# Two conditioning parts of a two-block kernel, summed on VectorE and TensorE instead of on TensorE alone

## The chip, the cores and the metric

The kernel runs on one core of one Trainium2 chip. The metric is the device time of one execution in microseconds, lower is better. The kernel before takes 1520.97 us, the median of three runs from 1515.06 to 1523.17. The one execution that was profiled took 1522.59 us, and its first to last instruction span 1520.8 us.

## The reference, cut to what matters

Two transformer blocks are computed for 256 tokens of width 1024 in float32. Each layer is conditioned on a vector `c`: a row vector of 1024 is multiplied with a 1024 x 6144 matrix, and the six pieces of 1024 shift, scale and gate the layer's stages.

```python
c_act = jax.nn.silu(c)
mod = c_act @ w_ada[layer] + b_ada[layer]
shift_m, scale_m, gate_m, shift_f, scale_f, gate_f = [m[:, None, :] for m in jnp.split(mod, N_MOD, axis=-1)]
h = rmsnorm(x, norm_mix[layer]) * (1.0 + scale_m) + shift_m
x = x + gate_m * hybrid_mixer(h, ...)
h = rmsnorm(x, norm_ffn[layer]) * (1.0 + scale_f) + shift_f
x = x + gate_f * hierarchical_moe(h, ...)
```

The first block's mixer has a projection, three kinds of recurrences and an output projection; a mixture of experts follows. The second block has two layers: a state-space and dilated-attention mixer with a SwiGLU, then a convolution with a SwiGLU.

## The kernel before, in words

There are three conditioning products (index `l`: 0 for the first block, 1 and 2 for the layers of the second). Each is cut into three parts (`b`) of 2048 columns, and each part into eight slices (`kt`) of 128 rows, so a slice is a tile of 128 x 2048 floats, 1 MB. `ada` (L484) takes one slice: for each of four groups of 512 columns one matmul multiplies the slice with a column of `c` broadcast to 32 columns, and the four groups land in the four 32-row strips of one PSUM bank (L498), which eight slices accumulate. The profile counts each such float32 matmul as two records, so a slice is 8 records of L498. After the eighth slice ScalarE copies the bank out (`adasb`, L504) and `ada_end` transposes it and adds the bias, some steps later.

The slices come in through the same ring as all dense weights: the class `Weights` keeps a list of jobs in the order in which they will be used, each one a load of up to 1 MB into one of five buffers (`rawa`, NA = 5), issued on SyncE's queue (L183). `pump` issues job i as soon as job i-5 has been marked free in program order, and the buffer that it takes is the one that was freed first. All loads are in one queue, so a load that waits for its buffer holds back those behind it. A dense weight's buffer is freed once it has been split: for each unit (128 x 1024) ScalarE writes a rounded high part (`whi`, L211), VectorE the rest (`wlo`, L212). Four units fit (`n_whl` = 4), so splits normally run one or two units ahead of the matmuls; `pump_units` stops where the next unit's raw load has not been issued yet. An `ada` slice's buffer is freed by `ws.free` (L500), as soon as its matmuls have been written down.

The work of one dense block (two units, 128 output columns each) is issued by `dense_B` (matmuls L627 to L629) or `dense_A` (L701 to L703). Inside it, `tick` is called four times per block; each tick advances every generator in `pipes` by one step, and so spreads the recurrences, the norms and the conditioning's ends between the matmuls. At the end of a block, `after` runs the slices that `spread` put there.

The first mixer's blocks are `fg` (2), `gq` (3), `vt` (4, by `dense_A`), `rqk` (3), `gate` (4) and the output projection. Part (0, 1) has its slices 0 | 1, 2 | 3, 4 after the blocks gq0, gq1 and gq2, its slices 5, 6 after vt0 and 7 after vt1; parts (0, 2) and (1, 0) follow, mostly two slices to a block. The job list around the change runs gq1, slices 1 and 2, gq2, slices 3 and 4, vt0, slices 5 and 6, vt1, slice 7 and the first of (0, 2), vt2, and so on. Meanwhile the forget gates, the transposes of the log gates and the recurrences (`recur`, L931, exponentials at L939, score masks at L980 to L991) run from the ticks.

Part (1, 2) belongs to the attention stage: its eight slices come after the blocks 0, 2, 4, ... 14 of the 18 `qkv` blocks. In the first half of this stage GpSimd loads position-bias tiles (`bt`, L1789 and L1793) with many small packets.

Of the kernel before, what the change touches and what calls it, by code (L numbers as in the profile page):

```python
# [11 lines left out]
FT = mybir.dt.float32  # L12
FR = mybir.dt.float32r
I32 = mybir.dt.int32
AF = mybir.ActivationFunctionType
OP = mybir.AluOpType
# [248 lines left out]
def trace(tc, A, out, dbg=None, stop=None):  # L265
    with ExitStack() as ctx:
        _trace(ctx, tc, A, out, dbg, stop)


def _trace(ctx, tc, A, out, dbg, stop):  # L270
    nc = tc.nc
    V, S, G, P = nc.vector, nc.scalar, nc.gpsimd, nc.tensor

    const = ctx.enter_context(tc.tile_pool(name="const", bufs=1))
# [14 lines left out]
    def acc(tag="acc"):  # L289
        n, pool = psums[tag]  # L290
        return pool.tile([128, 512], FT, name=tag, tag=tag, bufs=n)

    def mis():
        return acc("mis")

    NA, NB, NW = 5, 9, 2
    ws = Weights(nc)
# [5 lines left out]
    ada_at = {}  # L303

    HALVED = {(2, 2)}

    def plan_ada(l, b, kt):
        w, c = ada_w[l], b * 2048
        if (l, b) in HALVED:
            h, q = divmod(kt, 4)  # L310
            src, shape = w[q * 256:q * 256 + 256, c + h * 1024:c + h * 1024 + 1024], (2, 1024)
            src = src.rearrange("(k p) n -> p k n", p=128)
        else:
            src, shape = w[kt * 128:(kt + 1) * 128, c:c + 2048], (2048,)
        ws.add(("ada", l, b, kt), [(None, src)], shape)
# [85 lines left out]
    wk = l1.enter_context(tc.tile_pool(name="wk1", bufs=1))  # L401
# [27 lines left out]
    ones_1 = epsc[:, 1:2]  # L429
# [45 lines left out]
    cs = const.tile([128, 16], FT, name="cs")  # L475
    ps = mis()
# [4 lines left out]

    ada_ps = {}

    def ada(l, b, kt):  # L484

        h = 2 if (l, b) in HALVED else 1
        half, q = divmod(kt, 8 // h)
        if q == 0:
            ada_ps[0] = pada.tile([128, 512], FT, name="adaps", tag="adaps", bufs=1)
        w = 512 // h  # L490
        ps = ada_ps[0][:, :w]
        raw = ws.get(("ada", l, b, kt))
        if h == 1:
            raw = raw[:, None]
        col = (0 if l == 0 else 8) + q * h
        for k in range(h):
            for g in range(4):
                P.matmul(ps[32 * g:32 * g + 32, :], cs[:, col + k:col + k + 1].to_broadcast([128, 32]),  # L498
                         raw[:, k, g * w:(g + 1) * w], start=(q + k == 0), stop=(q * h + k == 7))
        ws.free(("ada", l, b, kt))  # L500
        if not ada_ends(l, b, kt):
            return
        sb = const.tile([128, 512], FT, name="adasb", tag="adasb", bufs=1)
        S.activation(sb[:, :w], ps, AF.Copy)  # L504
        pipes.append(ada_end(l, b * 16 + half * 8, 4 // h, sb))

    def ada_ends(l, b, kt):

        return kt % (4 if (l, b) in HALVED else 8) == (3 if (l, b) in HALVED else 7)

    def ada_end(l, n, w, sb):
        bias = vcol["b_ada"] if l == 0 else vcol["ada_b_2"][:, 48 * l - 48:48 * l]
        for _ in range(5):
            yield True
        tp = mis()
        for j in range(w):
            P.transpose(tp[:, j * 128:(j + 1) * 128], sb[:, j * 128:(j + 1) * 128], ident)
        o = mods[l][:, n:n + 4 * w].rearrange("p (g j) -> p g j", g=4)
        V.tensor_tensor(o, tp[:, :128 * w].rearrange("p (j g r) -> p g j r", g=4, r=32)[:, :, :, 0],
                        bias[:, n:n + 4 * w].rearrange("p (g j) -> p g j", g=4), op=OP.add)  # L520


    pipes = []
# [25 lines left out]
    class Squares:  # L549
# [6 lines left out]
        def add(self, t, scale=1.0):  # L556

            self.todo.append((t, scale))
            while self.todo and (len(self.todo) > 1 or self.n == 7):
                if 1 < self.n < 7:  # L560
                    V.tensor_tensor(self.sum, self.sum, self.end[-1], op=OP.add)
                t, scale = self.todo.popleft()
                sq = const.tile([128, T], FT, name="sq", tag="sq", bufs=2) if self.n else self.sum
                S.activation(sq, t, AF.Square, scale=scale)
                self.end = self.end[-1:] + [sq]
                self.n += 1
# [7 lines left out]
    def rsqrt(ms, scale=1.0, w=2, v=None):  # L574


        y, t = (const.tile([128, 12], FT, name="nw", tag="nw", bufs=9)[:, :w] for _ in range(2))
        if v is None:
            v = const.tile([128, 12], FT, name="nw", tag="nw", bufs=9)[:, :w]
            V.tensor_scalar(v, ms, scale, EPS, op0=OP.mult, op1=OP.add)  # L580
        V.tensor_scalar(y.bitcast(I32), v.bitcast(I32), -0.5, 1597463007.0, op0=OP.mult, op1=OP.add)
        for _ in range(3):
            V.tensor_tensor(t, y, y, op=OP.mult)
            V.scalar_tensor_tensor(t, t, -0.5, v, op0=OP.mult, op1=OP.mult)
            V.scalar_tensor_tensor(y, t, 1.5, y, op0=OP.add, op1=OP.mult)
        return y
# [44 lines left out]
    def after(name, b):  # L631
        last = False
        for k in ada_at.get((name, b), ()):
            if last:
                later(1, lambda k=k: ada(*k))
            else:
                ada(*k)
            last = last or ada_ends(*k)
# [87 lines left out]
    for kt in range(4):  # L726
        ada(0, 0, kt)
    ps = mis()
# [67 lines left out]


    w01 = wk.tile([128, C1OFF - o0], FT, name="w01", tag="sg")
    nc.sync.dma_start(w01, A["consts"][:, o0:C1OFF])
    G.tensor_copy(wlev, w01)  # L800
    nc.sync.dma_start(l1c, A["consts"][:, C1OFF:C1END])
# [269 lines left out]
    sg = wk.tile([128, 8, T], FT, name="sg", tag="sg")  # L1071
# [49 lines left out]
    with ExitStack() as l1:  # L1121
        wk = l1.enter_context(tc.tile_pool(name="wkm", bufs=1, reuse_waits="tile"))
# [48 lines left out]
        for kt in range(8):  # L1171
            if kt == 3:
                ps = mis()
# [67 lines left out]
        ps = mis()  # L1241
# [307 lines left out]
    with ExitStack() as l2:  # L1549
        hl = l2.enter_context(tc.tile_pool(name="hl2", bufs=1, reuse_waits="tile"))  # L1550
        dr = l2.enter_context(tc.tile_pool(name="dr2", bufs=1, space=bass.MemoryType.DRAM))
        wk = l2.enter_context(tc.tile_pool(name="wk2", bufs=1, reuse_waits="tile"))
# [7 lines left out]
        def yslab(tag, dt=FT):  # L1560
            return wk.tile([128, 8, T], dt, name=tag, tag=tag, bufs=2)
# [92 lines left out]
        ylo = []  # L1654
        yhi = [yslab("yh8", FR) for _ in range(2)]
        bcT = wk.tile([128, 8, T], FT, name="bcT")
        cw = vcol[("hy_conv_w_2")]
        cbm = wk.tile([128, 4, 3, 128], FT, name="cbm")
        Ub = cc("Uk")
# [329 lines left out]
    with ExitStack() as l3:  # L1989
        hl = l3.enter_context(tc.tile_pool(name="hl3", bufs=1, reuse_waits="tile"))  # L1990
        wk = l3.enter_context(tc.tile_pool(name="wk3", bufs=1, reuse_waits="tile"))
# [92 lines left out]
        ps = mis()  # L2084
# [9 lines left out]
        r = rsqrt(dl[:, 2:4])  # L2094
# [4 lines left out]
        ps = mis()  # L2099
# [33 lines left out]
    with ExitStack() as lf_:  # L2133
        wk = lf_.enter_context(tc.tile_pool(name="wko", bufs=1, reuse_waits="tile"))
        ps = acc()
        sq.mean(ps)
        r = rsqrt(ps[:, 0:2])
# [21 lines left out]
```

## Time and profile before

| | |
|---|---|
| median of three runs | 1520.97 us |
| the profiled execution | 1522.59 us, span 1520.8 us |
| TensorE matmul / weight load busy | 89% / 76% |
| VectorE / ScalarE / GpSimd busy | 56% / 42% / 17% |
| HBM traffic | 344.83 MB read, 227 GB/s over the span |
| L498, all nine conditioning parts | 77.5 us of TensorE, 640 records |
| first mixer, dense blocks gq to gate | about 62 to 236 us |
| attention stage, blocks qkv0 to qkv17 | about 760 to 927 us |

Times in the rows are counted from the span's start. Busy time is the time in which an engine had at least one instruction of that kind running; a bracket behind a timeline row gives the idle time before it and what ended that. PEld is TensorE's weight load, PEclk the share of full clock that TensorE was granted.

### The profile page before, as it was taken

To read this page: it belongs to the slowest core of one execution; us is meant where nothing else is said; L and a number is where in the kernel's file an instruction comes from. 1 tells how busy PE (TensorE), PEld (TensorE's weight loads), DVE (VectorE), ACT (ScalarE), POOL (GpSimd) and SP (SyncE) were. 2 spreads that over 40 slices of the span, in tenths; PEclk is the share of its full clock that TensorE was granted. 3 is DMA by queue.
4 is the path that set the end of the run, shared out by engine and by line. 5 is a ranking of instruction groups with operands and counts; after the bars stand their busy time and mean duration, and the time that the engine had idled before them with its cause. 6 is when DMAs were issued, how large, how long until landed. Compare 5 with 4: busy or idle time off the path is not lost.

```text
span 1520.8 us, 29127 instructions
## 1 busy us (share of the span) xinstructions
PE 1348.5 (89%) x12025; PEld 1156.3 (76%) x12025; DVE 851.7 (56%) x1727; ACT 645.5 (42%) x1164; POOL 253.6 (17%) x321
## 2 busy tenths in 40 slices
PE   3989899677766797999998898999999998999997
PEld 1777679544333596878986786899998987899997
DVE  3655555512211587787655565665555777765553
ACT  2543233210000365665343554454443776554432
POOL 3100000100000201034165106700000574000000
PEclk9898999798888798999999999999999999999999
DMA  8885577699999975676899966776557554877540
GB/s 310 273 304 190 174 237 281 273 417 386 410 418 419 223 171 175 208 242 197 201 173 176 248 194 194 220 196 181 173 179 234 164 180 139 250 195 192 171 164 28
DMA packets 277756, 348.22 MB, mean 229 GB/s; under 512 B 18521, under 2 KB 250448, under 8 KB 258672
## 3 DMA queue, kind: packets, MB, share of 16 engines
q1 hardware_dynamic: 264704, 334.81, 69.1%
q0 software_dynamic: 12160, 9.56, 4.4%
q8 instruction: 97, 1.59, 0.5%
q10 hardware_dynamic: 752, 1.91, 0.3%
q14 instruction: 43, 0.35, 0.1%
HBM read 344.83 MB, written 1.13 MB: 227 GB/s over the span
## 4 chain that ended last, share of the span: by engine, by line
PE 49%; DMA 11%; DVE 6%; issue 4%; POOL 2%; ACT 2%; DVEq 0%; POOLq 0%; SPq 0%; ACTq 0%
PE acc L627 14%; PE acc L628 14%; PE acc L629 14%; DMA bt<-rbd 2%; DMA rawb<-in_expert_w_up_dram 2%; DMA rawa<-in_hy_w_in_dram 2%; DVE wlo L212 2%; PE adaps L498 2%; POOL c L2029 1%; DMA rawb<-in_expert_w_gate_dram 1%; DMA rawa<-in_expert_w_down_dram 1%; PE acc L1380 1%; DMA rawa<-in_expert_w_up_dram 1%; DMA rawa<-in_expert_w_gate_dram 1%; ACT whi L211 1%
## 5 line engine op out<-in xcount | busy, mean ns | idle before, releaser
L627 PE MATMUL acc<-hhi,whi 128*128 128x256 f32 (+2 forms) x1728 | 511.9, 296 | 9.1 <-ACT hhi L617 5.4
L212 DVE TENSOR_TENSOR wlo<-rawa,whi 128x1024 fp32r<-128x1024 f32 (+1 forms) x303 | 370.0, 1225 | 256.2 <-ACT whi L211 253.5
L628 PE MATMUL acc<-hlo,whi 128*128 128x256 f32 (+2 forms) x1728 | 498.2, 288 | 1.6 <-DVE hlo L623 1.2
L629 PE MATMUL acc<-hhi,wlo 128*128 128x256 f32 (+2 forms) x1728 | 496.0, 287 | 1.3 <-DVE wlo L212 1.3
L211 ACT ACTIVATE whi<-rawa 128x1024 fp32r<-128x1024 f32 (+1 forms) x304 | 313.1, 1034 | 150.1 <-PE acc L628 106.5
L627 PEld LDWEIGHTS acc<-hhi,whi 128*128 128x128 f32 (+2 forms) x1728 | 336.8, 195 | 43.9 <-issue 22.5
L628 PEld LDWEIGHTS acc<-hlo,whi 128*128 128x128 f32 (+2 forms) x1728 | 337.2, 195 | 6.4 <-DVE hlo L623 4.2
L629 PEld LDWEIGHTS acc<-hhi,wlo 128*128 128x128 f32 (+2 forms) x1728 | 337.2, 195 | 2.0 <-DVE wlo L212 1.7
L627 PE MATMUL acc<-ghi,whi 128*128 128x256 f32 x352 | 100.1, 284 | 0.0
L628 PE MATMUL acc<-glo,whi 128*128 128x256 f32 x352 | 99.6, 283 | 0.0
L629 PE MATMUL acc<-ghi,wlo 128*128 128x256 f32 x352 | 99.6, 283 | 0.0
L498 PE MATMUL adaps<-rawa,cs 128*32 128x512 f32 (+1 forms) x640 | 77.5, 589 | 6.0 <-DMA rawa<-in_w_ada_dram 6.0
L1380 PE MATMUL acc<-rawb,X 128*32 128x256 f32 x576 | 64.3, 453 | 19.1 <-DMA rawb<-in_expert_w_gate_dram 10.9
L1979 POOL TENSOR_SCALAR dg<-cst,pcols 128x128 f32<-128x128 f32 x75 | 53.7, 734 | 84.3 <-PE acc L629 84.3
L628 PEld LDWEIGHTS acc<-glo,whi 128*128 128x128 f32 x352 | 67.6, 192 | 0.0
L629 PEld LDWEIGHTS acc<-ghi,wlo 128*128 128x128 f32 x352 | 67.6, 192 | 0.0
L627 PEld LDWEIGHTS acc<-ghi,whi 128*128 128x128 f32 x352 | 67.5, 192 | 0.0
L1388 DVE TENSOR_TENSOR sq<-sq,acc 128x256 f32<-128x256 f32 x8 | 3.4, 420 | 114.2 <-PE acc L1380 114.2
L1380 PEld LDWEIGHTS acc<-rawb,X 128*32 128x32 f32 x576 | 28.0, 129 | 43.7 <-DMA rawb<-in_expert_w_gate_dram 16.4
L1380 PE MATMUL acc<-rawa,X 128*32 128x256 f32 x320 | 41.5, 451 | 21.5 <-DMA rawa<-in_expert_w_up_dram 11.4
L1793 POOL DMA_DIRECT2D bt<-rbd x64 | 51.0, 813 | 30.2 <-DMA bt<-rbd 30.1
L627 PE MATMUL acc<-yh,whi 128*128 128x256 f32 x192 | 54.8, 286 | 0.0
(597 smaller groups left out, 2179.3 us busy)
## 6 DMA issues: line engine op xcount, KB each, us to landing
rawa<-in_ada_w_dram SPq DMA_DIRECT2D x48, 1024.0 KB, 5.2
rawa<-in_w_ada_dram SPq DMA_DIRECT2D x24, 1024.0 KB, 8.3
rawa<-in_ffn_w_gate_dram SPq DMA_DIRECT2D x44, 512.0 KB, 4.1
rawa<-in_ffn_w_up_dram SPq DMA_DIRECT2D x44, 512.0 KB, 5.4
rawa<-in_hy_w_in_dram SPq DMA_DIRECT2D x20, 1024.0 KB, 5.5
rawa<-in_hy_w_in_dram SPq DMA_DIRECT2D x40, 512.0 KB, 7.7
rawb<-in_expert_w_gate_dram SPq DMA_DIRECT2D x18, 1024.0 KB, 19.9
rawb<-in_expert_w_up_dram SPq DMA_DIRECT2D x18, 1024.0 KB, 16.3
```

Of the source, the lines that this page charges most:

```text
L211: self.nc.scalar.activation(hv, src, AF.Copy)
L212: (engine or self.nc.vector).tensor_tensor(lv, src, hv.bitcast(FT), op=OP.subtract)
L498: P.matmul(ps[32 * g:32 * g + 32, :], cs[:, col + k:col + k + 1].to_broadcast([128, 32]), raw[:, k, g * w:(g + 1) * w], start=(q + k == 0) ...
L627: P.matmul(ps, wh, xh, start=start, stop=False)
L628: P.matmul(ps, wh, xl, start=False, stop=False)
L629: P.matmul(ps, wl, xh, start=False, stop=stop)
L1380: P.matmul(ps[32 * i:32 * i + 32, :256], X[:, kt, o:o + 32], half(raws[i], kt // 4)[:, kt % 4 * 256:kt % 4 * 256 + 256], start=(kt == 0), ...
L1388: V.tensor_tensor(hid, s, out_[1][:, :256], op=OP.mult)
L1793: nc.gpsimd.dma_start(bt[:, a, o + 64 * g:o + 64 * g + 64], bass.AP(tensor=rbd.tensor, offset=base + 511 + 127 * g, ap=[[0, 2], [1, 64], [ ...
L1979: G.tensor_scalar(diag[n][:, i], ident, tap(i, n), None, op0=OP.mult)
L2029: G.tensor_tensor(c2, c2, pr_, op=OP.add)
```

## The change

For the two parts (0, 1) and (1, 2) the sum over the 1024 rows is made in two steps. Each slice is multiplied by its column of `c`, as a per-partition scalar, and added into a 128 x 2048 float32 tile `asum` on VectorE, in four instructions of 512 columns (the first slice by `tensor_scalar`, the other seven by `scalar_tensor_tensor`, in place). The four instructions are steps of a generator, one to a tick, so that they fall into the block after the one that the slice stood behind, and `ws.free` of the slice's buffer follows the fourth. Two ticks after the last slice's fourth step, four matmuls with a column of ones, broadcast to 32 columns, sum `asum` over the partitions into a PSUM bank of the pool `mis`; the copy to `adasb` and `ada_end` are as before. `asum` takes the memory of the tag `sg` in the first mixer and of `bcT` in the attention stage. The other seven parts are unchanged.

```diff
     HALVED = {(2, 2)}
+    SUMMED = {(0, 1), (1, 2)}
...
+    def ada_summed(l, b, kt):
+
+        raw = ws.get(("ada", l, b, kt))
+        col = cs[:, (0 if l == 0 else 8) + kt:(0 if l == 0 else 8) + kt + 1]
+        if kt == 0:
+            asums[l, b] = asums[l, b]()
+        t = asums[l, b]
+
+        def add():
+            for g in range(4):
+                r = slice(g * 512, g * 512 + 512)
+                if kt == 0:
+                    V.tensor_scalar(t[:, r], raw[:, r], col, None, op0=OP.mult)
+                else:
+                    V.scalar_tensor_tensor(t[:, r], raw[:, r], col, t[:, r], op0=OP.mult, op1=OP.add)
+                if g < 3:
+                    yield True
+            ws.free(("ada", l, b, kt))
+            if kt < 7:
+                return
+            yield True
+            yield True
+            ps = mis()
+            for g in range(4):
+                P.matmul(ps[32 * g:32 * g + 32, :], ones_1.to_broadcast([128, 32]), t[:, g * 512:(g + 1) * 512], start=True,
+                         stop=True)
+            sb = const.tile([128, 512], FT, name="adasb", tag="adasb", bufs=1)
+            S.activation(sb, ps, AF.Copy)
+            pipes.append(ada_end(l, b * 16, 4, sb))
+        pipes.append(add())
+
     def ada(l, b, kt):
 
+        if (l, b) in SUMMED:
+            ada_summed(l, b, kt)
+            return
...
-        return kt % (4 if (l, b) in HALVED else 8) == (3 if (l, b) in HALVED else 7)
+        return (l, b) not in SUMMED and kt % (4 if (l, b) in HALVED else 8) == (3 if (l, b) in HALVED else 7)
...
+    asums[0, 1] = lambda wk=wk: wk.tile([128, 2048], FT, name="asum", tag="sg")
...
+        asums[1, 2] = lambda: wk.tile([128, 2048], FT, name="asum", tag="bcT")
```

## Rows read from the trace of the kernel before

**Rows 1.** The page's first part: busy time and share of each engine.
```profile
PE 1348.5 (89%) x12025; PEld 1156.3 (76%) x12025; DVE 851.7 (56%) x1727; ACT 645.5 (42%) x1164; POOL 253.6 (17%) x321
```

**Rows 2.** Busy time by stretch, first mixer; columns as the header row says.
```profile
core 0: us, PE busy (x) PEld busy (x) DVE busy (x) ACT busy (x) POOL busy (x), PEclk, DMA share, GB/s
70.00:84.00 14.00, 14.00 (x118) 10.82 (x118) 9.57 (x21) 8.06 (x12) 0.00 (x0) 1.00 0.72 266
84.00:94.00 10.00, 10.00 (x75) 8.04 (x75) 5.33 (x12) 4.61 (x8) 0.00 (x0) 1.00 0.95 322
94.00:106.00 12.00, 12.00 (x280) 10.69 (x284) 6.71 (x25) 4.18 (x6) 0.00 (x0) 1.00 0.83 275
106.00:112.00 6.00, 2.30 (x20) 1.49 (x12) 4.63 (x12) 1.98 (x11) 0.00 (x0) 1.00 0.90 328
112.00:120.00 8.00, 7.88 (x138) 6.43 (x142) 1.82 (x3) 2.09 (x10) 0.00 (x0) 0.52 0.01 3
120.00:128.00 8.00, 8.00 (x147) 6.06 (x140) 4.18 (x5) 3.10 (x8) 0.00 (x0) 0.84 0.67 223
190.00:236.00 46.00, 45.86 (x382) 36.02 (x382) 25.49 (x64) 15.47 (x31) 0.00 (x0) 1.00 0.66 218
```

**Rows 3.** Timeline of TensorE, the conditioning slices of the first mixer: start, length.
```profile
73.27 1.92 PE L498 MATMUL adaps<-rawa,cs 128*32 128x512 f32 x16
82.03 1.92 PE L498 MATMUL adaps<-rawa,cs 128*32 128x512 f32 x16
92.07 1.92 PE L498 MATMUL adaps<-rawa,cs 128*32 128x512 f32 x16
105.61 1.06 PE L498 MATMUL adaps<-rawa,cs 128*32 128x512 f32 x8
128.89 1.92 PE L498 MATMUL adaps<-rawa,cs 128*32 128x512 f32 x16
```

**Rows 4.** Timeline of SyncE's queue: raw loads of vt0, vt1, vt2; first expert loads.
```profile
74.39 0.38 SPq L183 DMA_DIRECT2D rawa<-in_w_in_dram  x1
83.17 1.00 SPq L183 DMA_DIRECT2D rawa<-in_w_in_dram  x2
93.11 1.47 SPq L183 DMA_DIRECT2D rawa<-in_w_in_dram  x2
...
236.83 3.93 SPq L183 DMA_DIRECT2D rawb<-in_expert_w_gate_dram  x4
```

**Rows 5.** Timelines of VectorE and ScalarE: the splits around vt0 and vt1.
```profile
74.58 1.23 DVE L212 TENSOR_TENSOR wlo<-rawa,whi 128x1024 fp32r<-128x1024 f32 x1 [0.50 <-ACT whi L211]
80.78 2.36 DVE L212 TENSOR_TENSOR wlo<-rawa,whi 128x1024 fp32r<-128x1024 f32 x2 [3.56 <-ACT whi L211]
...
79.68 2.01 ACT L211 ACTIVATE whi<-rawa 128x1024 fp32r<-128x1024 f32 x2 [3.17 <-DMA rawa<-in_w_in_dram]
87.93 1.09 ACT L939 ACTIVATE X<-mis 128x512 f32<-128x512 f32 x2 [4.72 <-PE mis L938]
89.63 2.01 ACT L211 ACTIVATE whi<-rawa 128x1024 fp32r<-128x1024 f32 x2 [0.61 <-DMA rawa<-in_w_in_dram]
```

**Rows 6.** Single VectorE lines, ns min/median/max: the nearest shapes to the new instructions.
```profile
L846 DVE SCALAR_TENSOR_TENSOR gk<-E,lbt,s x3: 479/483/483, 72.8 to 73.6; 128x256 f32<-128x256 f32 x3
L1192 DVE SCALAR_TENSOR_TENSOR ht<-acc,nw,brow x2: 741/742/744, 280.0 to 280.6; 128x512 f32<-128x512 f32 x2
L841 DVE TENSOR_SCALAR L<-L x1: 561/561/561, 72.2 to 72.2; 128x768 f32<-128x768 f32 x1
```

**Rows 7.** Timeline of TensorE: the first matmul behind the gap in vt2.
```profile
112.12 0.39 PE L701 MATMUL acc<-whi,hhi 128*128 128x256 f32 x1 [3.82 <-ACT vtok L902]
```

**Rows 8.** Busy time by stretch, attention stage (columns as in group 2); ScalarE's waits, 764 to 848.
```profile
788.00:848.00 60.00, 48.58 (x400) 39.98 (x398) 28.40 (x77) 23.79 (x50) 32.55 (x42) 0.91 1.17 168
848.00:908.00 60.00, 59.42 (x532) 50.82 (x529) 39.70 (x114) 33.77 (x70) 0.00 (x0) 1.00 0.84 237
...
ACT whi L211 <- DMA rawa<-in_hy_w_in_dram: 22.4, 6, 7.7
```

More of the change, by code (lines that the diff above doesn't have):

```diff
@@ L482, in _trace @@
     ada_ps = {}
+    asums = {}
+    def ada_summed(l, b, kt):
[26 more added lines that the diff above has]
+        pipes.append(add())
     def ada(l, b, kt):
+        if (l, b) in SUMMED:
+            ada_summed(l, b, kt)
+            return
         h = 2 if (l, b) in HALVED else 1
```

## The prediction

> **What bounds the kernel now.** I read the page's first part, then the busy time by stretch over the two stages that the change touches, then in each the queue that ends the waits. Over the whole run TensorE's matmuls are busy 1348.5 us, VectorE 851.7 [rows 1]. That alone speaks for the change: work moves from a full engine to one with room. But the room must be where the work lands. In the first mixer TensorE is busy in every microsecond from 70 to 106 [rows 2], and VectorE in 9.57 of 14, 5.33 of 10 and 6.71 of 12 us. The loads are tight there as well: ScalarE's split of vt0 waited 3.17 us for its load, that of vt1 0.61 us [rows 5], at a DMA share up to 0.95 [rows 2]. SyncE's rows show why. The load of vt1 goes out at 83.17 and that of vt2 at 93.11 [rows 4], just when VectorE's split of vt0 ends (80.78 + 2.36 = 83.14 [rows 5]): a ring of five buffers with none to spare, in which every load waits for a buffer of a block or two earlier. The attention stage has two halves. From 788 to 848 TensorE is idle for 11.4 of 60 us, the DMA share is 1.17 and ScalarE waited 22.4 us for raw weights: transfers bound it. From 848 to 908 TensorE is busy 59.42 of 60 us [rows 8].
>
> **Prices.** Removed: two slices take 1.92 us of TensorE [rows 3], 0.96 us each, 16 of them. Added: the four matmuls with ones have the shapes of one slice, at most 1.06 us [rows 3], once per part. Added on VectorE: 28 `scalar_tensor_tensor` per part. The nearest rows are 0.483 us for 256 elements in SBUF and 0.742 us for 512 elements with a PSUM source [rows 6]; I take 0.70, near the second, since the element count is the same. The four `tensor_scalar` lie under the 0.561 us of 768 elements [rows 6]; I take 0.5. A part is 28 x 0.70 + 4 x 0.5 = 21.6 us of VectorE.
>
> **The first mixer, gq to vt0.** The steps of slice 0 fall into gq1, those of slices 1 and 2 into gq2: 2.0 + 8 x 0.70 = 7.6 us, where VectorE has 14 - 9.57 = 4.4 us free [rows 2]. That is over-full by 3.2 us. What matters more is the ring. Counted through the job list, the buffers freed before vt0's load are gq1's, gq2's and slice 0's; slices 3 and 4 take the first two, vt0 the third. That buffer is now free after slice 0's fourth step. VectorE reaches these steps behind the split that ends at 74.58 + 1.23 = 75.81 [rows 5]. With 2.0 us of their own and some 1.4 us of other work (9.57 us in 14 less 1.23 and 2.36 of splits is 0.43 per us) the fourth ends at 79.2. So the load leaves at 79.2 instead of 74.39, lands 79.68 - 74.39 = 5.3 us later, at 84.5, and is split by 1.0 us of ScalarE and 1.23 of VectorE. VectorE is by then working off the eight steps of slices 1 and 2 (5.6 us from 79.2) and about 2 us of other work, to 86.8. vt0 begins at about 87.9; before, it began at 82.03 + 1.92 = 83.95 [rows 3]. That is +4.0 us, after the saving of all five slices ahead of it; +2 if VectorE's queue is empty, +6 if more stands in it. The five slices, 4.8 us, buy only idle time.
>
> **The clock.** TensorE is then idle from 82.03 - 3 x 0.96 = 79.15 to 87.9. The one gap of that kind in this stage is 3.82 us at 112.12 [rows 7]; behind it the granted clock is 0.52 over 112 to 120 and 0.84 over 120 to 128 where it was 1.00 [rows 2], the 1.2 GHz level for most of it: 8 x 0.48 + 8 x 0.16 = 5.1 us of work lost. I take 5.1 for this longer gap; bounds 0 and 5.1 for each later one.
>
> **vt0 to vt3.** A split can only be written down once its load has been issued, and issue now follows the fourth steps at the end of a block. So the splits of vt1, vt2 and vt3, which stood inside the block before, come behind that block, and vt0's own second unit comes in the middle of vt0, behind ScalarE's exponentials (1.09 us [rows 5]), which wait for matmuls of that block. Queued behind these waits on ScalarE and VectorE are the evacuations and masks of the recurrence.
> Second unit of vt0: 1.0 + 1.2 us and the rest of an exponential, +3.0 (1.0 to 3.3).
> vt1: its load takes vt0's buffer, so it leaves after that second split, then 89.63 - 83.17 = 6.5 us of transfer and 2.2 of splitting, against half a block of matmuls, (92.07 - 83.95) / 2 = 4.1 us: 4.6 idle, less slices 5 and 6 (1.92) that are no longer there, +2.7. While the clock is low the half block is longer and hides some of this; I take back 2.5.
> vt2: split behind vt1, 2.2 us and about 1 of queue, less slice 7 and the first slice of (0, 2), which now fills the wait: +1.2. Against that, the old gap of 3.82 us came from ScalarE waiting behind VectorE's mask work, and that work gets its time while vt1 waits for its load: -3.8, and of its clock loss half, -2.5 (0 to -5.1).
> vt3: the same 3.2 us less 1.92 under two slices of (0, 2), +1.3. The ones: +1.06.
> VectorE's 11.2 us of steps in vt0 and vt1 meet 5.33 + 6.71 us of work in 22 us [rows 2]: over-full by 1.2, +1.2.
> Sum: 4.0 + 5.1 + 3.0 + 2.7 - 2.5 + 1.2 - 6.3 + 1.3 + 1.06 + 1.2 = +10.8 us; with the bounds +3 to +19. From rqk0 on, the order of loads and splits is the old one. The stretch before the experts has no slack to give it back (45.86 of 46 us busy [rows 2]), and the experts' loads begin at its end, at 236.83 [rows 4]. The shift goes through.
>
> **The attention stage.** Here one slice stands at every second block, and the same count through the job list shows each raw load waiting for a buffer that comes free at about the old time; the order of the splits is unchanged. Four of the eight slices lie before 848, where transfers set the pace: their removal I cost at a gain of nothing, covered by the 11.4 idle us. The other four save 3.84 us, the ones cost 1.06, and VectorE's steps (10.8 us into 59.42 - 39.70, about 20 us free [rows 8]) hold up some transposes; I take +1.0. Net -1.8; bounds -6.6 (all eight slices count, nothing is held up) and +4.
> The weight loads of TensorE are busy 50.82 of those 60 us [rows 8], less than its matmuls. [...]
>
> **Sum.** +10.8 - 1.8 = +9.0 us. On the profiled execution's own 1522.59 us that is 1531.6; the median of the runs is 1.6 us below it, so the forecast for a median is 1530.0 us.
>
> **Rivals.** (1) The lateness is absorbed: vt0 starts only 2 us late, no clock loss there, and the old gap goes with its whole clock loss: 2 + 3.0 + 2.7 + 1.2 - 8.9 + 1.3 + 1.06 = +2.4, less 1.8, 1521.6 us. For it: the old gap has the cause that I say. Against: the load of vt0 cannot leave before slice 0's steps.
> (2) Faster: TensorE's relief decides. If VectorE works the steps off without holding up loads or splits, 12 of the 16 slices count (four stay under the transfers), 11.5 - 2.1 = 9.4 us, 1511.6 us. It decides as soon as vt0's load leaves before about 75 us, that is if slice 0's four steps run ahead of the split at 74.58. For it: 44% of VectorE's time is free [rows 1]. Against: not between 70 and 84.
> (3) Each gap costs clock: the waits in vt0 and ahead of vt1 and vt2 are 3 to 5 us too, the size of the one gap that did. Two more at 5.1 give 1540.2 us. The Trainium skill, TensorE: Matmul & The Clock Gate, HAM oscillation, describes just such a loop, matmuls broken by waits for transfers, that falls back to the low clock at each wait; the trace of before shows it once [rows 7].
>
> **How the numbers follow.** Forecast 0.56, rival (1) 0.20, (2) 0.09, (3) 0.15. The range leaves out the ends of (2) and (3) and takes in the bounds in between: 1515 to 1540. A measurement can tell about 0.5%, 7.6 us: below 1513.4 is faster, 0.09; above 1528.6 is slower, 0.34 of the forecast's 0.56 and (3), 0.49; in between 0.42.
>
> **What would show it.** vt0's raw load near 79 us instead of 74.39; a gap of 5 us or more on TensorE ahead of vt0 and a low clock behind it; the second unit's split behind the exponentials; vt1's load some 10 us or more after vt0's start; experts' loads near 248 instead of 236.83; the attention stage within 3 us of its old length. If the experts' loads begin before 237, the mixer part is wrong; if VectorE's steps take 0.5 us or less, the over-full windows go.

## The result, and the profile after

The changed kernel takes 1537.4 us (median), the kernel before 1519.3 us in the runs beside it: the ratio is 1.0116, interval 1.0097 to 1.0135, so 17.6 us slower (14.7 to 20.5). The profiled execution of after took 1538.15 us with a span of 1536.4, against 1520.8. The forecast was 1530.0, slower, within 1515 to 1540: direction and range held, the size was half of what came.

The page's first part of after, to be read against [rows 1]:

```profile
PE 1344.1 (87%) x11913; PEld 1161.5 (76%) x11913; DVE 892.8 (58%) x1791; ACT 645.6 (42%) x1164; POOL 254.7 (17%) x321
```

Sixteen slices left TensorE and two sets of ones came, some 13 us less work, but its busy time fell only by 4.4 us. The mean granted clock of the span is 0.937 instead of 0.942, and what is left runs longer where it is lower; that this is the whole difference is not shown. The new lines, single instructions, ns min/median/max:

```profile
L499 DVE TENSOR_SCALAR asum<-rawa,cs x8: 468/479/693, 77.3 to 794.4; 128x512 f32<-128x512 f32 x8
L501 DVE SCALAR_TENSOR_TENSOR asum<-rawa,cs,asum x56: 733/746/753, 79.9 to 928.4; 128x512 f32<-128x512 f32 x56
L511 PE MATMUL mis<-asum,epsc x16: 592/604/616, 147.8 to 931.9; 128*32 128x512 f32 x16
```

So a part's single steps add up to 28 x 0.746 + 4 x 0.479 = 22.8 us, where 21.6 was forecast; back to back they overlap a little, so the two parts lengthen VectorE's busy time by 41.1 us, not 45.6. Busy time by stretch in the first mixer of after (columns as in [rows 2]; whole programs are compared, so the stretches are not the same work):

```profile
70.00:84.00 14.00, 10.42 (x86) 9.98 (x85) 12.70 (x28) 7.88 (x12) 0.00 (x0) 1.00 0.43 146
84.00:94.00 10.00, 5.75 (x24) 5.28 (x25) 6.22 (x10) 1.06 (x1) 0.00 (x0) 0.66 0.61 228
94.00:106.00 12.00, 6.12 (x38) 4.84 (x36) 10.45 (x25) 5.11 (x8) 0.00 (x0) 1.00 0.58 186
106.00:112.00 6.00, 5.63 (x27) 5.13 (x28) 4.48 (x7) 2.14 (x6) 0.00 (x0) 0.72 0.96 311
112.00:120.00 8.00, 8.00 (x259) 6.89 (x257) 6.81 (x21) 1.55 (x6) 0.00 (x0) 1.00 0.07 16
120.00:128.00 8.00, 4.24 (x24) 3.52 (x17) 5.80 (x8) 3.40 (x10) 0.00 (x0) 0.79 0.78 265
...
70.00:144.00 74.00, 55.39 (x754) 47.26 (x754) 55.52 (x113) 27.98 (x60) 0.00 (x0) 0.91 0.57 194
```

From 70 to 106 TensorE was never idle before [rows 2]; now it is for 13.7 of 36 us. VectorE is nearly full from 70 to 84. Over 70 to 144 TensorE idles for 18.6 us. What it waited for there (timeline of TensorE after, rows behind a gap and, last, the two slices that stand ahead of vt3; L738 and L739 are the vt matmuls with the high and the low part of the split, before L701 and L702):

```profile
78.14 0.39 PE L664 MATMUL acc<-hhi,whi 128*128 128x256 f32 x1 [1.71 <-DVE gq L930]
87.54 0.58 PE L738 MATMUL acc<-whi,hhi 128*128 128x256 f32 x1 [5.40 <-ACT whi L211]
...
97.08 0.38 PE L738 MATMUL acc<-whi,hhi 128*128 128x256 f32 x1 [1.66 <-ACT whi L211]
98.34 0.38 PE L739 MATMUL acc<-wlo,hhi 128*128 128x256 f32 x1 [0.88 <-DVE wlo L212]
105.11 0.39 PE L738 MATMUL acc<-whi,hhi 128*128 128x256 f32 x1 [2.84 <-ACT whi L211]
...
123.41 0.38 PE L738 MATMUL acc<-whi,hhi 128*128 128x256 f32 x1 [2.88 <-ACT whi L211]
...
138.84 1.92 PE L535 MATMUL adaps<-rawa,cs 128*32 128x512 f32 x16
```

Every long gap is a wait for a split: ahead of vt0, inside vt0, ahead of vt1, ahead of vt2. The old gap behind `vtok` [rows 7] is gone. SyncE's queue of after shows the loads behind these splits, to be read against [rows 4]:

```profile
79.83 0.38 SPq L183 DMA_DIRECT2D rawa<-in_w_in_dram  x1
...
98.31 1.01 SPq L183 DMA_DIRECT2D rawa<-in_w_in_dram  x2
...
107.47 1.01 SPq L183 DMA_DIRECT2D rawa<-in_w_in_dram  x2
...
249.53 3.93 SPq L183 DMA_DIRECT2D rawb<-in_expert_w_gate_dram  x4
```

vt0's load leaves 5.4 us later than before, vt1's 15.1, vt2's 14.4, the experts' 12.7. Of these, 1.3 us stand already ahead of the first step of the change, as one early matmul shows in the timelines of TensorE before and after:

```profile
59.33 0.69 PE L826 MATMUL mis<-gaT,wa 16*128 16x256 f32 x2 [0.46 <-ACT gaT L865]
```

```profile
60.63 0.69 PE L864 MATMUL mis<-gaT,wa 16*128 16x256 f32 x2 [0.46 <-ACT gaT L903]
```

So the mixer is 11.4 us longer (249.53 - 60.63 against 236.83 - 59.33). The spans differ by 15.6 us; the other 2.9 came later. By SyncE's loads, an input stage of the second block that the change does not touch is 2.4 us longer, and so is the attention stage (from its first raw load to the first of the SwiGLU behind it, 744.35 to 951.42 against 729.49 to 934.18); about 1.6 us are won back behind that and 0.3 in the experts.

### The profile page after: what moved, and what is told of

Read it like the earlier page. It is cut to its first block, busy times and chain, and to the rows that moved or that the text cites. A ratio compares the mean times of both kernels' runs of the same rounds, so it can differ in the third digit from the quotient of the medians.

```text
span 1536.4 us, 28963 instructions
## 1 busy us (share of the span) xinstructions
PE 1344.1 (87%) x11913; PEld 1161.5 (76%) x11913; DVE 892.8 (58%) x1791; ACT 645.6 (42%) x1164; POOL 254.7 (17%) x321
## 4 chain that ended last, share of the span: by engine, by line
PE 60%; DMA 17%; DVE 11%; issue 5%; ACT 4%; POOL 2%; ACTq 0%; DVEq 0%; POOLq 0%; SPq 0%
PE acc L664 15%; PE acc L665 14%; PE acc L666 14%; DMA rawa<-in_hy_w_in_dram 4%; DMA rawb<-in_expert_w_gate_dram 3%; DVE wlo L212 3%; DMA rawa<-in_expert_w_up_dram 3%; PE acc L1418 3%; PE adaps L535 3%; ACT whi L211 2%; POOL c L2068 1%; DMA rawb<-in_expert_w_up_dram 1%; DMA bt<-rbd 1%; DMA xrow<-in_x_dram 1%; DMA rawa<-in_expert_w_down_dram 1%
## 5 line engine op out<-in xcount | busy, mean ns | idle before, releaser
L1418 PE MATMUL acc<-rawb,X 128*32 128x256 f32 x576 | 65.8, 455 | 18.4 <-DMA rawb<-in_expert_w_gate_dram 10.9
L535 PE MATMUL adaps<-rawa,cs 128*32 128x512 f32 (+1 forms) x512 | 61.3, 589 | 6.5 <-DMA rawa<-in_w_ada_dram 6.5
L1418 PEld LDWEIGHTS acc<-rawa,X 128*32 128x32 f32 x320 | 18.9, 131 | 48.6 <-DMA rawa<-in_expert_w_up_dram 16.6
## 6 DMA issues: line engine op xcount, KB each, us to landing
rawb<-in_expert_w_up_dram SPq DMA_DIRECT2D x18, 1024.0 KB, 15.4
```

What stands on the lines that cost most here:

```text
L1418: P.matmul(ps[32 * i:32 * i + 32, :256], X[:, kt, o:o + 32], half(raws[i], kt // 4)[:, kt % 4 * 256:kt % 4 * 256 + 256], start=(kt == 0), ...
```

## The experiments

Each kernel is compared with the kernel before on its own chip; the differences are the ratios of the runs times 1520 us. Rows come from one profiled execution of each kernel: that of e4 took 1522.10 us, 4.3 below the median of its runs, that of e3 1534.66, 5.5 above. So the runs say how much a kernel costs, the rows where it waits.

| kernel | what it has | ratio, interval | us |
|---|---|---|---|
| the change | both parts | 1.0116, 1.0097 to 1.0135 | +17.6 (14.7 to 20.5) |
| e1_part01 | mixer's part alone | 1.0094, 1.0059 to 1.0129 | +14.3 (9.0 to 19.6) |
| e2_part12 | attention's part alone | 1.0011, 0.9995 to 1.0028 | +1.7 (-0.8 to 4.3) |
| e3_free_late | late buffers, slices on TensorE | 1.0067, 1.0045 to 1.0090 | +10.2 (6.8 to 13.7) |
| e4_vector_only | VectorE's steps, slices on TensorE | 1.0054, 1.0037 to 1.0071 | +8.2 (5.6 to 10.8) |
| e10_both_kept | both costs, slices on TensorE | 1.0082, 1.0063 to 1.0101 | +12.5 (9.6 to 15.4) |
| e6_relief01 | mixer's slices left out, no cost | 0.9959, 0.9945 to 0.9972 | -6.2 (-8.4 to -4.3) |
| e7_relief12 | attention's slices left out, no cost | 1.0000, 0.9986 to 1.0015 | 0.0 (-2.1 to 2.3) |
| e5_at_once | both parts, steps at once | 1.0077, 1.0060 to 1.0093 | +11.7 (9.1 to 14.1) |
| e13_at_once01 | mixer's part, buffer held 0 ticks | 1.0059, 1.0043 to 1.0076 | +9.0 (6.5 to 11.6) |
| e14_two_ticks | mixer's part, buffer held 2 ticks | 1.0058, 1.0039 to 1.0076 | +8.8 (5.9 to 11.6) |

**Which part.** e1 and e2 name one part each in `SUMMED`.

```diff
-    SUMMED = {(0, 1), (1, 2)}
+    SUMMED = {(0, 1)}
```

> The changed kernel with only part (0, 1) of the first mixer summed on VectorE; part (1, 2) of the attention stage is as before. Theory (late buffers: each raw buffer is held until the fourth step, so loads and splits of vt0 to vt3 come late and TensorE waits): the first mixer loses what it lost with the whole change, +11 to +13 us at the experts' first loads (near 248 to 250 instead of 236.83), and the total is 11 to 15 us above the kernel before. Rival (the whole change's 18 us come in equal parts from both conditioning parts): total +7 to +10, with the experts' loads near 245.

> The changed kernel with only part (1, 2) of the attention stage summed on VectorE; the first mixer is as before. Theory (the prediction's working for this stage, and its length in the two traces): the attention stage is -2 to +3 us longer, the total within -3 to +4 us of the kernel before, experts' loads near 237. Rival (both parts cost the same): total +7 to +10 us.

The mixer's part alone costs 14.3 us, attention's 1.7, which can't be told from nothing; together 16.0 against 17.6 for the whole. The rival, equal shares, is out.

**Late buffers alone, VectorE's steps alone.** e3 is the kernel before with this edit:

```diff
-        ws.free(("ada", l, b, kt))
+        if (l, b) == (0, 1):
+            def free_late():
+                for _ in range(3):
+                    yield True
+                ws.free(("ada", l, b, kt))
+            pipes.append(free_late())
+        else:
+            ws.free(("ada", l, b, kt))
```

> The kernel before, with TensorE still summing all slices, but each raw buffer of part (0, 1) is given back at the fourth tick behind its slice instead of at once; VectorE gets no added work. Theory (late buffers): the order of loads and splits is that of the changed kernel, so most of the mixer's loss shows without any VectorE step: vt0's raw load at 76 to 80 us instead of 74.39, gaps on TensorE ahead of vt0 to vt3, experts' loads near 245 (242 to 250), total +8 us (+4 to +13). Rival (VectorE's queue is too full and holds up splits and evacuations; the order of the loads matters little): total within 2 us of the kernel before, experts' loads 236 to 239.

e4 is the kernel before with steps on a spare tile that do not read the slices, the buffers freed as before (the lines that set up the tile are left out here):

```diff
...
+            def steps():
+                for g in range(4):
+                    r = slice(g * 512, g * 512 + 512)
+                    if kt == 0:
+                        V.memset(t[:, r], 1.0)
+                    else:
+                        V.scalar_tensor_tensor(t[:, r], xT.rearrange("p k t -> p (k t)")[:, r], c0, t[:, r], op0=OP.mult, op1=OP.add)
+                    if g < 3:
+                        yield True
+            pipes.append(steps())
```

> The kernel before, with TensorE still summing all slices and the raw buffers given back at once, plus 32 VectorE steps of the change's size at the change's ticks (four fills and 28 scalar_tensor_tensor on a spare tile, whose result nobody reads). Theory (late buffers): the loads keep their order, vt0's load leaves at 74 to 77 us, experts' loads 237 to 241, total +1 to +4 us. Rival (VectorE's queue alone): the mixer loses +8 us or more, experts' loads at 245 or later, total +8 to +13.

Late buffers alone cost 10.2 us, as the theory said. But VectorE's steps alone cost 8.2, which the theory (+1 to +4) had not: both are causes. The largest gap of after, the 5.40 us ahead of vt0, is in neither. In e3 vt0's load left at 75.34 (76 to 80 was expected), 15.05 us behind the early matmul, in e4 at 72.40, 15.03 behind it, as before (15.06); in after it is 19.20. That gap needs steps that read the slices, so that the load waits for them. The two kernels leave different traces. Timeline of TensorE in e3, rows behind a gap:

```profile
91.96 0.39 PE L708 MATMUL acc<-whi,hhi 128*128 128x256 f32 x1 [1.65 <-ACT whi L211]
...
118.01 0.58 PE L708 MATMUL acc<-whi,hhi 128*128 128x256 f32 x1 [2.88 <-ACT whi L211]
```

These are two of the gaps of after, 1.66 and 2.88 us, to within 0.01 us, without a single step on VectorE. The 2.84 us ahead of vt1 are not among e3's gaps: there TensorE still works on slices 5 and 6. Timeline of TensorE in e4, rows behind a gap, and its busy time around them:

```profile
87.55 0.50 PE L957 MATMUL mis<-wlev,lfl 128*128 128x512 f32 x1 [1.89 <-DVE lfl L875]
...
115.79 0.58 PE L719 MATMUL acc<-whi,hhi 128*128 128x256 f32 x1 [6.37 <-ACT vtok L921]
```

```profile
94.00:106.00 12.00, 11.74 (x267) 10.49 (x263) 11.86 (x27) 4.19 (x6) 0.00 (x0) 1.00 0.77 264
106.00:112.00 6.00, 2.93 (x33) 1.85 (x33) 5.89 (x22) 0.67 (x4) 0.00 (x0) 0.95 0.80 265
112.00:120.00 8.00, 4.21 (x103) 3.65 (x106) 4.44 (x7) 2.19 (x11) 0.00 (x0) 0.50 0.16 65
120.00:128.00 8.00, 8.00 (x172) 5.45 (x162) 4.83 (x6) 3.13 (x7) 0.00 (x0) 0.69 0.22 63
```

Here the loads of vt0 and vt1 are on time (81.12 for vt1, 23.75 us behind the early matmul, 23.84 before), and the old wait behind `vtok` is longer: 6.37 us instead of 3.82 [rows 7], with VectorE busy 11.86 of 12 and 5.89 of 6 us ahead of it, working off steps between the score masks. The granted clock behind it is 0.50 over 112 to 120, the 1.2 GHz level, and 0.69 over 120 to 128, where before it was 0.52 and 0.84 [rows 2].

**What the relief of TensorE is worth.** e6 and e7 leave out slices 0 to 6 of one part:

```diff
-        for k in range(h):
+        left = (l, b) == (0, 1)
+        for k in range(0 if left and kt < 7 else h):
...
```

> The kernel before, with the matmuls of slices 0 to 6 of part (0, 1) left out (their loads stay, and buffers come free at once), and nothing put in their place: part (0, 1) of the conditioning is not summed here. It takes 28 of its 32 matmuls, 7 x 0.96 = 6.7 us, from TensorE, and so shows what the relief alone can give in this stage. Theory (the ring of loads sets the pace there, so relief buys idle time): 0 to -3 us. Rival (TensorE sets the pace): -5 to -7 us, experts' loads at 230 to 232 instead of 236.83.

> The kernel before, with the matmuls of slices 0 to 6 of part (1, 2) left out (loads stay), and nothing put in their place: part (1, 2) of the conditioning is not summed here. Theory (the prediction's: four of the slices lie where transfers set the pace): -2 to -4.5 us. Rival (all count): -6 to -7 us. Second rival (none counts, the stage waits for VectorE and ScalarE throughout): 0 to -1.5 us.

Both theories fell, in opposite directions. In the mixer 6.7 us of matmuls left out give 6.2 us, with the experts' loads at 226.79 us (the early matmul at 58.84): TensorE does set the pace there as long as nothing is held up. (e6 also gives the buffers back without a reader, and vt0's load leaves 10.2 us behind the early matmul instead of 15.1; the two effects are not taken apart, but before, TensorE waited for nothing from 70 to 106 [rows 2].) In the attention stage the same 6.7 us give nothing. Busy time of its second half in e7, and in e2, where VectorE's steps are added; before it was 59.42 of 60 us [rows 8]:

```profile
848.00:908.00 60.00, 56.73 (x495) 50.60 (x495) 40.66 (x114) 33.60 (x72) 0.00 (x0) 0.97 0.79 228
```

```profile
848.00:908.00 60.00, 55.03 (x483) 49.71 (x482) 46.67 (x125) 32.06 (x68) 0.00 (x0) 0.97 0.74 210
```

Four slices less are 59.42 - 3.84 = 55.6 us; e2 shows 55.03 (in e7, which keeps the last slice, three less are 56.5, and 56.73 are shown). What was taken from TensorE turned into idle time, most of it behind `pT` on ScalarE (3.0 of 3.3 us in e7, 4.4 of 5.0 in e2). SyncE's loads say the same: from the raw load at 855.42 to the first of the SwiGLU at 934.18 it is 78.8 us before, in e7 856.68 to 935.16, 78.5 us, with 2.9 us of matmuls left out. The first half is 5.1 us longer in e7's profile, and ScalarE waits 30.7 us for raw weights there (22.4 before [rows 8]); why is open. A TensorE busy for 99% of a stretch was not what set its length. That agrees with the Trainium skill (Perfetto Trace Analysis, Identifying the Most-Contended Engine), by which the busy share of matmuls "is not a good measure of how close you are to roofline". The weight loads, which it offers instead, were busy for 50.82 of these 60 us [rows 8], and even their 85% promised more than came.

e10 adds both costs in the mixer and keeps TensorE's slices beside them:

> The changed kernel for part (0, 1) alone, with TensorE's own slices kept beside it: VectorE does the change's 32 steps on the raw slices into a spare tile that nobody reads, each buffer is given back at the fourth step, and TensorE still sums all slices. It adds both costs and takes no relief. Theory (the relief of TensorE bought nothing beside late buffers): within 3 us of the kernel with part (0, 1) alone, so +14 to +20 us above the kernel before. Rival (the relief did pay, 6.6 us of TensorE): +21 to +25 us.

12.5 us with the slices kept, 14.3 without them, within the 3 us of the theory (though below its +14) and far from the rival's +21: TensorE did 6.6 us more work in e10, and it is not slower. Busy time from 70 to 144 us in e10 and in e1:

```profile
70.00:144.00 74.00, 63.10 (x818) 49.91 (x818) 55.85 (x116) 27.52 (x59) 0.00 (x0) 0.91 0.58 197
```

```profile
70.00:144.00 74.00, 55.80 (x704) 48.92 (x703) 51.48 (x105) 22.85 (x49) 0.00 (x0) 0.79 0.53 178
```

TensorE is idle for 10.9 us with the slices, 18.2 without: the 7.3 us between them are the relief, all of it idle. And both costs together (12.5) are less than their sum (10.2 + 8.2 = 18.4), by 5.9 us, which is little more than the intervals of the three allow: they hide behind each other, at least in part.

**How long a buffer is held.** In e5 the four steps stand behind each other where the slice stands, for both parts, and the buffer is freed behind them. e13 is that for the mixer's part alone, and e14, for that part too, has two steps to a tick:

```diff
-                if g < 3:
+                if g == 1:
                     yield True
...
```

> The changed kernel with the four VectorE steps of a slice written down at once, behind the block that the slice stands at, and its buffer given back right behind them, for both parts; the ones follow as late as before. Theory (two causes, each about half: late buffers cost about 10 us, VectorE's added work about 7): the raw loads and splits get their old order back, the added work stays, now in bursts of up to 8 x 0.73 = 5.9 us ahead of the splits; experts' loads at 241 to 246, total +7 to +12 us above the kernel before. Rival 1 (late buffers alone): +4 us or less, experts' loads 238 to 241. Rival 2 (the bursts are as bad as the late buffers): +15 us or more, experts' loads from 248 on.

> The changed kernel with part (0, 1) alone, its four steps per slice written down at once and the buffer given back right behind them; part (1, 2) as before. With the kernel that holds each buffer for four ticks (about 14 us above the kernel before) and the next run, a row of three holding times: 0, 2 and 4 ticks. Theory (VectorE's added work costs its 8 us whatever the holding time, the late buffers' part grows with it): +7 to +11 us. Rival (bursts cost as much as holding): +13 us or more.

> The changed kernel with part (0, 1) alone, two steps of a slice to a tick, so that its buffer is given back at the second tick instead of the fourth; part (1, 2) as before. Theory: between the neighbours, +9 to +13 us, with vt0's raw load between 75.6 and 79.8 us. Rival (a threshold: any hold into the next block puts the load behind the same splits): as with four ticks, +13 to +17 us.

Held for 0, 2 and 4 ticks the part costs 9.0, 8.8 and 14.3 us. The first two are equal, so the cost does not grow with the holding time as the theory had it, and the rival's threshold is there but at another place: the step lies behind the second tick, as far as e1's interval, which begins at 9.0, allows to say so. The first two show the gap behind `vtok`, as e4 does; with four ticks the waits for splits stand in its place. But both also wait ahead of vt0, which e4 does not, for there the steps read the slices (timeline of TensorE, rows behind a gap; e13, then e14):

```profile
84.66 0.58 PE L738 MATMUL acc<-whi,hhi 128*128 128x256 f32 x1 [3.06 <-ACT whi L211]
...
116.34 0.58 PE L738 MATMUL acc<-whi,hhi 128*128 128x256 f32 x1 [5.76 <-ACT vtok L940]
```

```profile
85.76 0.58 PE L738 MATMUL acc<-whi,hhi 128*128 128x256 f32 x1 [3.45 <-ACT whi L211]
...
119.29 0.58 PE L738 MATMUL acc<-whi,hhi 128*128 128x256 f32 x1 [6.63 <-ACT vtok L940]
```

The loads of vt1 (SyncE's queue; e13, e14, then e1) tell the same:

```profile
87.02 1.00 SPq L183 DMA_DIRECT2D rawa<-in_w_in_dram  x2
```

```profile
88.13 1.00 SPq L183 DMA_DIRECT2D rawa<-in_w_in_dram  x2
```

```profile
96.88 1.00 SPq L183 DMA_DIRECT2D rawa<-in_w_in_dram  x2
```

From the early matmul of each (57.34, 58.86, 59.28 us) that is 29.7, 29.3 and 37.6 us; before, 83.17 - 59.33 = 23.8. Two ticks change nothing in the order of the splits, four push vt1's load behind vt0's second split. With the buffers freed at once about 9 us remain, near the 8.2 of e4. That they are the same 8 us is not shown: e13 and e14 have the wait ahead of vt0 and a TensorE with less to do, e4 has neither. For the whole change the same step brings +17.6 down to +11.7 (e5, with the experts' loads at 240.24, just ahead of the 241 to 246 that were expected).

The mixer's length from the early matmul to the experts' first load, one execution each, falls into the same groups: 182.4, 182.7 and 182.6 us in e13, e14 and e4, 186.5 and 186.2 in e3 and e10, 188.9 and 195.0 in the change and e1. Where nothing is touched in it (before, e2, e7) it takes 177.5, 175.3 and 174.2.

## Why the prediction was right, and why it was half the size

**The ring.** The mechanism was right: vt0's load left at 79.83, right behind slice 0's fourth step, which ended at 79.80 (timeline of VectorE after):

```profile
79.32 0.48 DVE L499 TENSOR_SCALAR asum<-rawa,cs 128x512 f32<-128x512 f32 x1
```

Less the 1.3 us of the start, that is 78.5, where 79.2 was forecast. vt0 began at 87.54, so at 86.2, where 87.9 was forecast: it came 2.3 us later than before, not 4.0. The second unit's split stands behind the exponentials (timeline of ScalarE after, against [rows 5]):

```profile
86.43 1.06 ACT L211 ACTIVATE whi<-rawa 128x1024 fp32r<-128x1024 f32 x1 [3.66 <-DMA rawa<-in_w_in_dram]
...
95.00 1.09 ACT L977 ACTIVATE X<-mis 128x512 f32<-128x512 f32 x2 [7.51 <-PE mis L976]
95.97 1.06 ACT L211 ACTIVATE whi<-rawa 128x1024 fp32r<-128x1024 f32 x1
```

That cost 1.66 + 0.88 = 2.5 us of TensorE (3.0 forecast). vt1's load left 10.8 us after vt0's start (10 or more). vt2 waited 2.88, and the old gap behind `vtok` went, as said. The slices ahead of vt3 stand at 138.84 against 128.89 [rows 3]: 9.95 less the 1.30 of the start is +8.65, where the terms up to there, without vt3's, add up to +8.4. At the experts' loads the profile says +11.4 for the mixer, the sum said +10.8. That they agree so well is in part luck: vt0's term was 1.7 us too large, and the next paragraph shows how much both profiles of the mixer can vary.

**The clock.** Three of the waits are followed by a lower clock: 0.66 over 84 to 94, 0.72 over 106 to 112, 0.79 over 120 to 128, in sum 3.4 + 1.7 + 1.7 = 6.8 us at most (in the first of them TensorE was busy for 5.75 of 10 us only), where before 5.1 were lost. Forecast was +2.6, found at most +1.7; rival (3) had the pattern right (a drop behind each wait, as the Trainium skill, TensorE: Matmul & The Clock Gate, HAM oscillation, describes for waits on transfers), but each drop was smaller than its 5.1 us. Its full price shows in another execution. e1 runs the same program in the mixer, and there the stretch from 128 to 144, where after has 1.00, reads

```profile
128.00:144.00 16.00, 16.00 (x268) 14.16 (x268) 5.62 (x9) 3.06 (x11) 0.00 (x0) 0.53 0.38 131
```

0.47 x 16 = 7.5 us. e1's mixer is 254.30 - 59.28 = 195.0 us long (its experts' loads were expected near 248 to 250), that of after 188.9, 6.1 us apart. So +11.4 is one draw for this stage and +17.5 another, and the 14.3 us of e1's runs lie between. The mixer of before is a draw too, the longest of the three in which nothing was touched, and with it the old gap, 3.82 us there [rows 7] but less in e2 and e7 (timeline of TensorE; e2, then e7):

```profile
110.95 0.39 PE L738 MATMUL acc<-whi,hhi 128*128 128x256 f32 x1 [2.50 <-ACT vtok L940]
```

```profile
110.91 0.38 PE L702 MATMUL acc<-whi,hhi 128*128 128x256 f32 x1 [2.53 <-ACT vtok L903]
```

So two terms of the sum are mis-sized, as far as these profiles tell. The clock's 2.6 us came from a single gap of one execution, and the upper bound of +19 left no room for a drop behind vt2 or vt3; e1 lost 7.5 us there, over 128 to 144. And the credit of 3.8 us for the old gap, with its clock loss on top, was read from the execution in which that gap was longest; 2.5 is what two others show.

**VectorE over-full.** This step gave a cause the wrong size: I gave VectorE's full queue 1.2 us beside what it does to vt0. Alone it costs 8.2 (e4), and 9 with the buffers freed in time (e13). It did not show in the sum because, with late buffers, TensorE waits for the splits anyway (e10: 12.5 for both, 10.2 for late buffers alone). A reader who had freed the buffers in time by my account would have expected a loss of a few microseconds and got +9 (e13).

**"The five slices buy only idle time."** Right beside the late buffers (e10 against e1), but the mixer does pay for relief, 6.2 us (e6), when nothing else is late. Rival (2)'s mechanism was sound there and its condition was not met: not even with steps at once does vt0's load leave before 75 us (75.54 in e13, whose early matmul stands 2.0 us sooner than that of before).

**The attention stage.** Forecast -1.8, measured +1.7 (-0.8 to 4.3). The step that failed is "the other four save 3.84 us", read from 59.42 busy of 60 us [rows 8]: relief is worth 0.0 (e7). With a gain of nothing, ones of 1.06 and VectorE's hold-up of 1.0 the same sum gives +2.1; the profiles of after and e2 have the stage 2.4 and 2.8 us longer than before (207.1 and 207.5 us against 204.7 by SyncE's loads).

**The sum.** Forecast +9.0, measured +17.6. The runs of single parts account for it so: mixer 14.3 instead of 10.8, attention 1.7 instead of -1.8, and 1.6 left, less than the intervals. What stays open: whether the 1.6 is anything, and how the 14.3 divides between clock and waits in the executions that were not profiled. A sixth raw buffer, which might undo the lateness and keep the quarter steps, wasn't tried.

## What to carry to other kernels

Before moving work off a busy engine, leave the work out on the chip: it gave 6.2 us in one stage and nothing in another, in whose second half TensorE was busy for 99% of the time. A consumer moved to a later place in the order holds its input buffer longer; count what is loaded and split next through that buffer, and check separately whether the receiving engine has room at that very place, for removing one of two causes gives back only what the other doesn't also cost.

## What the runs showed of the hardware that was not expected

- The same program got different clocks in different executions behind the same gap of 2.88 us ahead of vt2: 1.00 (after) and 0.53 (e1) of full clock over 128 to 144 us, in stages that differ by 6.1 us of 190. Even the untouched mixer of before, e2 and e7 differs by 3.3 us from profile to profile (177.5, 234.10 - 58.83 = 175.3 and 232.74 - 58.52 = 174.2), so one trace does not settle a term of a few microseconds.
- `scalar_tensor_tensor` of 128 x 512 floats, all operands in SBUF and in place, takes 0.746 us, no less than the 0.742 of the same size with a PSUM source [rows 6].
- 6.6 us of matmuls added to a stage with waits (e10 against e1) cost nothing that could be measured; the mean granted clock over 70 to 144 was 0.91 with them and 0.79 without, though after, without them too, also had 0.91.
